# Attends drawn together, head sums in two float32r parts, an affine moved to ScalarE and two PSUM banks exchanged, in a hybrid decoder layer

## The chip, the cores and the metric

One core of a Trainium2 chip. The metric is the device time of one execution in microseconds (us); less is better. TensorE (PE) multiplies, PEld loads its stationary operands, VectorE (DVE), ScalarE (ACT) and GpSimd (POOL) work on elements, SyncE (SP) issues most of the DMAs. All run at the same time and wait for each other by semaphores.

## The reference

One decoder layer for 256 tokens of width 2048 in float32: a SwiGLU feed-forward part (5632 wide), a mixer of sliding-window attention beside RWKV-7 time mixing, cross-attention into 256 memory tokens, a second feed-forward part and a final norm. The change lies in the mixer, whose attention has 16 heads of 64, 4 key/value heads and blocks of 128, and whose time mixing has 16 heads of 64:

```python
def sliding_window_attention(q, k, v, sinks):
    ...
    s = jnp.einsum('bnqhgd,bnkhd->bnhgqk', qb, kb).astype(jnp.float32) * (HEAD_DIM ** -0.5)
    ...
    m = jnp.maximum(jnp.max(s, axis=-1, keepdims=True), sink)
    e = jnp.exp(s - m)
    p = e / (jnp.sum(e, axis=-1, keepdims=True) + jnp.exp(sink - m))
    o = jnp.einsum('bnhgqk,bnkhd->bnqhgd', p.astype(v.dtype), vb)

def rwkv7_time_mix(p, mu, w0, w2, a0, a2, g2, k_k, k_a, r_k, ln_w, ln_b):
    ...
    w_log = -jax.nn.softplus(-(w0.astype(f32) + jnp.tanh(xw) @ w2.astype(f32))) - 0.5
    a = jax.nn.sigmoid(a0.astype(f32) + xa @ a2.astype(f32))
    g = jax.nn.sigmoid(xg) @ g2.astype(f32)
    ...
    kk = k * k_k
    kk = kk / jnp.maximum(jnp.sqrt(jnp.sum(kk * kk, axis=-1, keepdims=True)), 1e-12)
    k = k * (1.0 + (a - 1.0) * k_a)
    y = rwkv7_scan(r, decay, k, v, -kk, kk * a)
```

kk are the removal keys; their squares are summed over each head's 64 columns.

## The kernel before

All weights stream from HBM through `load` (SP's DMAs). Each piece of 2x128 rows by 512 columns is split by ACT into a float32r part (`hi`, L365) and by DVE into the rest (`lo`, L366). Each product of a weight column block takes three float32r matmuls for each k and each 128 tokens: L442 (hi by hi), L443 and L444 (the two cross terms). These are the "plain" matmuls below; they fill most of the run. `product` issues them and calls `bg.tick()` between steps. The mixer's own work is written as generators in the queues of `Interleave`: at each tick every queue lets its first one or two generators run to their next `yield`, so `idle(n)` shifts work by n ticks. What a generator issues thus stands between plain matmuls in each engine's instruction order, and each engine runs its own order, one after the other.

PSUM has eight banks in three rings: `acc` (3, the products), `mm` (3) and `tr` (2, transposes and small results). A ring's bank is taken again when its last reader is done. SBUF tiles of the mixer come from a pool of 23 buffers (tag "t4").

The parts that the change touches, with the lines of before:

- `attend(kv)`, for each of four key/value heads, two at a time: scores (L954, query block 0 in two tr banks, block 1 in two mm banks) to tiles `s` (DVE, L962), maximum and exponential (ACT, L984), division (DVE, L993), transposes of the probabilities (L1003) through tr banks and ACT's copies to `pt` (L1007), output (L1014) in a tr bank, and its parts `yahi` (ACT, L1024) and `yalo` (DVE, L1025). For kv = 1 and 3 it idles five ticks first.
- `decay_and_rate`, when all four are done issuing ("attn"): it loads `wa`, the second rank weights of the decay and the rate, by two DMAs on POOL (L1078, L1079), applies Tanh and Sigmoid (L1081, L1082) to the small features xwa and xg, multiplies (L1091, mm and tr banks) and applies Sigmoid (L1098). The Sigmoid of xg also feeds DMAs of `gate_parts` on POOL (L1144), which copy rows of xg.
- `removal_keys(h)`, for each half of the heads: squares of kk on ACT (L1174), sums over a head by a matmul with block ones (L1179, float32), square root (ACT, L1180), maximum and reciprocal (DVE, L1182, L1184), the affine of the rate `aa` (DVE, L1202), products with it (L1206, L1207), and the masked products `lt` (L1224). `head_sums` (L906) is the helper that other sums use: two float32r matmuls, for a float32r part and the rest.
- the main stream beside it multiplies the gates and w_proj_attn and forms `ga` (DVE, L1271) from an acc bank.
- `pairs(h, q)`, the chunks of the recurrence (scores L1348, masks L1356, outputs L1459 and L1464), and `finish(h, i)` with the gate's product (L1523).

## Time and profile before

| what | value |
|---|---|
| median of three runs | 2225.18 us (2224.05 to 2226.93) |
| the profiled execution | 2226.33 us |
| its span in the profile | 2224.6 us |
| PE, DVE, ACT, POOL busy | 99%, 82%, 56%, 5% |
| HBM traffic | 209 GB/s over the span |

A row of the table by stretch holds the stretch and its length, then for PE, PEld, DVE, ACT and POOL the busy time and in brackets the instructions, then the granted clock of TensorE, the DMA engines' busy share and GB/s. A row of a timeline holds start, time (from the first's start to the last's end), engine, line, operation, output and input, tile size, shape and count; in brackets at its end the engine's idle time before it and what ended it. Matmuls overlap, so the distance between starts and not the time of one is what a matmul costs. A row of the waits holds the waiting group, what it waited for, total, number and longest, in us.

### The profile page before, as it was taken

What the parts mean: (1) busy time and instruction counts of PE and PEld (TensorE: products, weight loads), DVE (VectorE), ACT (ScalarE), POOL (GpSimd) and SP (SyncE); (2) the same over time, 40 slices, a digit from 0 to 9 for tenths busy, and PEclk for the clock granted to TensorE, in tenths of its full rate; (3) what the DMA queues carried; (4) which work ended last, traced back from release to release, by engine and by line L of the source; (5) the groups of instructions that cost most, each with busy time, mean ns of one, the idle gap of its engine ahead of it and who ended that gap; (6) DMA issues with size and microseconds to landing.
All of it is one profiled execution on the core that took longest, in us unless ns stands there. A gap on an engine that the chain in (4) does not pass through costs nothing.

```text
span 2224.6 us, 28133 instructions
## 1 busy us (share of the span) xinstructions
PE 2206.0 (99%) x10520; PEld 1819.2 (82%) x10520; DVE 1831.3 (82%) x2354; ACT 1244.2 (56%) x1611; POOL 107.2 (5%) x185
## 2 busy tenths in 40 slices
PE   9999999999999999999999999999999999999998
PEld 7888888888888877788888888888888888888886
DVE  7999988898989476978657666558999999999997
ACT  7555555555556467544544546556665565655654
POOL 0000000000000001000221030001000000000000
PEclk9999999999999999999999999999999999999999
DMA  8565555555556545676678678548565565656573
GB/s 304 194 209 198 194 203 199 201 191 202 203 192 202 175 126 149 191 235 209 205 236 293 203 265 281 186 157 288 206 234 189 197 247 204 208 208 218 199 242 137
DMA packets 231560, 466.02 MB, mean 209 GB/s; under 512 B 15520, under 2 KB 17920, under 8 KB 231424
## 3 DMA queue, kind: packets, MB, share of 16 engines
q1 hardware_dynamic: 222256, 438.08, 58.0%
q0 software_dynamic: 7648, 23.52, 3.5%
q10 hardware_dynamic: 1520, 2.63, 0.3%
q8 instruction: 82, 1.34, 0.2%
q14 instruction: 54, 0.44, 0.1%
HBM read 440.49 MB, written 23.59 MB: 209 GB/s over the span
## 4 chain that ended last, share of the span: by engine, by line
PE 94%; DVE 2%; DMA 1%; issue 1%; ACT 1%; SPq 0%; POOL 0%; POOLq 0%; DVEq 0%; ACTq 0%
PE acc L442 19%; PE acc L443 19%; PE acc L444 19%; PE mm L443 8%; PE mm L444 8%; PE mm L442 8%; PE tr L443 2%; PE tr L630 2%; PE tr L442 2%; PE tr L444 2%; PE mm L1418 1%; DVE lo L366 1%; DMA raw<-in_ffn_w_up_dram 0%; ACT hi L365 0%; DMA raw<-in_ffn_w_gate_dram 0%
## 5 line engine op out<-in xcount | busy, mean ns | idle before, releaser
L365 ACT CAST hi<-raw 128x1024 fp32r<-128x1024 f32 (+1 forms) x768 | 754.9, 993 | 698.3 <-PE acc L444 493.6
L366 DVE TENSOR_TENSOR lo<-raw,hi 128x1024 fp32r<-128x1024 f32 (+1 forms) x768 | 880.7, 1150 | 291.7 <-ACT hi L365 288.9
L442 PE MATMUL acc<-hi,xhi 128*128 128x512 f32 (+1 forms) x1134 | 448.1, 396 | 2.8 <-DVE ga L1271 1.3
L443 PE MATMUL acc<-lo,xhi 128*128 128x512 f32 (+1 forms) x1134 | 440.6, 389 | 0.8 <-DVE lo L366 0.8
L444 PE MATMUL acc<-hi,xlo 128*128 128x512 f32 (+1 forms) x1134 | 440.5, 389 | 0.0
L442 PEld LDWEIGHTS acc<-hi,xhi 128*128 128x128 f32 x1134 | 213.3, 188 | 49.2 <-issue 3.6
L443 PEld LDWEIGHTS acc<-lo,xhi 128*128 128x128 f32 x1134 | 213.6, 188 | 44.2 <-DVE lo L366 2.1
L444 PEld LDWEIGHTS acc<-hi,xlo 128*128 128x128 f32 x1134 | 213.2, 188 | 44.1 <-issue 0.8
L373 ACT CAST thi<-raw 128x1024 fp32r<-128x1024 f32 x192 | 200.2, 1051 | 67.5 <-DVE raw L396 44.1
L374 DVE TENSOR_TENSOR tlo<-raw,thi 128x1024 fp32r<-128x1024 f32 x192 | 232.5, 1219 | 0.9 <-ACT thi L373 0.3
L442 PE MATMUL mm<-hi,xhi 128*128 128x512 f32 x402 | 156.5, 389 | 0.0
L443 PE MATMUL mm<-lo,xhi 128*128 128x512 f32 x402 | 156.5, 389 | 0.0
L444 PE MATMUL mm<-hi,xlo 128*128 128x512 f32 x402 | 156.4, 389 | 0.0
L444 PE MATMUL acc<-hi,hlo 128*128 128x512 f32 x372 | 145.4, 391 | 0.0
L443 PE MATMUL acc<-lo,hhi 128*128 128x512 f32 x372 | 145.3, 391 | 0.0
L442 PE MATMUL acc<-hi,hhi 128*128 128x512 f32 x372 | 145.0, 390 | 0.0
L442 PEld LDWEIGHTS mm<-hi,xhi 128*128 128x128 f32 x402 | 75.5, 188 | 16.2 <-ACT hi L365 0.5
L443 PEld LDWEIGHTS mm<-lo,xhi 128*128 128x128 f32 x402 | 75.5, 188 | 15.8
L444 PEld LDWEIGHTS mm<-hi,xlo 128*128 128x128 f32 x402 | 75.5, 188 | 15.7
L442 PEld LDWEIGHTS acc<-hi,hhi 128*128 128x128 f32 x372 | 69.9, 188 | 14.3
L443 PEld LDWEIGHTS acc<-lo,hhi 128*128 128x128 f32 x372 | 69.8, 188 | 14.2
L444 PEld LDWEIGHTS acc<-hi,hlo 128*128 128x128 f32 x372 | 69.9, 188 | 14.1
(421 smaller groups left out, 3527.9 us busy)
## 6 DMA issues: line engine op xcount, KB each, us to landing
raw<-in_ffn_w_down_dram SPq DMA_DIRECT2D x88, 1024.0 KB, 5.2
raw<-in_ffn_w_gate_dram SPq DMA_DIRECT2D x84, 1024.0 KB, 5.0
raw<-in_ffn_w_up_dram SPq DMA_DIRECT2D x78, 1024.0 KB, 5.9
raw<-in_w_in_dram SPq DMA_DIRECT2D x136, 512.0 KB, 3.7
raw<-in_w_out_dram SPq DMA_DIRECT2D x32, 512.0 KB, 4.6
raw<-sums SPq DMA_DIRECT2D x20, 512.0 KB, 6.3
raw<-in_w_proj_attn_dram SPq DMA_DIRECT2D x16, 512.0 KB, 4.1
raw<-in_w_proj_rwkv_dram SPq DMA_DIRECT2D x16, 512.0 KB, 5.3
```

The lines of the kernel that those rows point to most:

```text
L365: at["hi"] = act.copy(hi[:, s], raw[:, s])
L366: at["lo"] = dve.tensor_tensor(lo[:, s], raw[:, s], f32(hi[:, s]), ALU.subtract)
L373: act.copy(hi[:], v[:])
L374: dve.tensor_tensor(lo[:], v[:], f32(hi[:]), ALU.subtract)
L442: pe.matmul(o, xh, hi, start=first, stop=False, **how)
L443: pe.matmul(o, xh, lo, start=False, stop=False, **how)
L444: pe.matmul(o, xl, hi, start=False, stop=last, **how)
L630: pe.transpose(b[:, o : o + P], tok[:, t, col : col + P], ident[:])
L1418: pe.matmul(vb[to, (o + k) * P : (o + k + 1) * P][:, r], lhs(k, e), v[:, k, r], start=v is u and k + e == 0, stop=True, **ek,)
```

## The change

Seven edits. `attend(3)` no longer idles five ticks (only kv = 1 does); ahead of the transposes attend(0) idles five ticks and the others three. The scores s of the first query block, which need half a buffer, and its probabilities pt share one t4 buffer, so that an attend takes three rather than four. `decay_and_rate` idles five ticks between the DMAs of wa and the Tanh. The sums of the squares take `head_sums`: ACT casts the squares to a float32r part, DVE forms the rest, and two float32r matmuls stand for one in float32. The affine of aa goes from DVE to ACT. One bank in `pairs` (h = q = 1, c = 0) and one in `finish(0, 0)` come from mm rather than tr, and `finish` idles one tick rather than two there.

```diff
--- before.py
+++ after.py
@@ -942,11 +942,16 @@
             if kv == 0:
                 with tc.issue_after(at["features"].ins):
                     act.activation(junk_t[:, :1], ones[:, :1], AF.Exp)
-            yield from idle(5 * (kv % 2))
+            yield from idle(5 * (kv == 1))
             s, b = [], []
             for qb, bank in enumerate((tr, mm)):
                 w, tq = P * (qb + 1), slice(qb * P, qb * P + P)
-                s.append(t4("s", (P, 2, 2, T)))
+                both = t4("s", (P, 2, 2, T))
+                if qb == 0:
+                    both = both[:].rearrange("p a b c -> p (a b c)")
+                    pt = [both[:, 4 * P :].rearrange("p (k i q) -> p k i q", k=1, i=4)]
+                    both = both[:, : 4 * P].rearrange("p (e c w) -> p e c w", e=2, c=2)
+                s.append(both)
                 b.append([bank() for _ in range(2)])
                 for c in range(2):
                     for e in range(2):
@@ -993,10 +998,9 @@
                     dve.tensor_scalar(
                         s3[qb][:, i], s3[qb][:, i], den[:, qb, i : i + 1], None, ALU.mult
                     )
-            yield from idle(3)
-            pt = []
+            yield from idle(5 if kv == 0 else 3)
+            pt.append(t4("pt", (P, 2, 4, P)))
             for qb in range(2):
-                pt.append(t4("pt", (P, 2, 4, P)))
                 for kb in range(qb + 1):
                     t_ = tr()
                     for i in range(4):
@@ -1077,6 +1081,7 @@
             wa = t4("wa", (P, RW))
             pool.dma_start(wa[0:64, :], W["rwkv_w2"])
             pool.dma_start(wa[64:128, :], W["rwkv_a2"])
+            yield from idle(5)
             with tc.issue_after(at["exp"].ins):
                 act.activation(xwa[0:64, :], xwa[0:64, :], AF.Tanh)
                 act.activation(xg[:], xg[:], AF.Sigmoid)
@@ -1166,17 +1171,19 @@
             yield from wait_for(f"k{h}")
             yield from wait_for("decay")
             ei = cs[h]
-            kk, sq = t4("kk"), t4("sq")
+            kk, sq, hi, lo = t4("kk"), t4("sq"), t4("sqhi", dt=F32R), t4("sqlo", dt=F32R)
             for i in range(4):
                 c = 4 * h + i
                 act.activation(kk[:, i, :], kt[h][:, i, :], AF.Copy, scale=nk_k[:, c : c + 1])
             yield
             act.activation(sq[:], kk[:], AF.Square)
+            halves_of(sq[:], hi[:], lo[:])
             yield
             for i in (0, 2):
-                b = tr()
                 sq2 = sq[:, i : i + 2, :].rearrange("p c t -> p (c t)")
-                pe.matmul(b[:], bdones[:], sq2, start=True, stop=True)
+                b = head_sums(
+                    bdones_r, [v[:, i : i + 2, :].rearrange("p c t -> p (c t)") for v in (hi, lo)]
+                )
                 act.activation(sq2, b[:], AF.Sqrt)
                 yield
                 dve.tensor_scalar(sq2, sq2, 1e-12, None, ALU.max)
@@ -1199,9 +1206,9 @@
             yield
             for i in range(4):
                 c = 4 * h + i
-                dve.tensor_scalar(
-                    aa[h][:, i, :], aa[h][:, i, :], k_a[:, c : c + 1], ok_a[:, c : c + 1],
-                    ALU.mult, ALU.add,
+                act.activation(
+                    aa[h][:, i, :], aa[h][:, i, :], AF.Identity, scale=k_a[:, c : c + 1],
+                    bias=ok_a[:, c : c + 1],
                 )
             dve.tensor_tensor(kt[h][:], kt[h][:], aa[h][:], ALU.mult)
             dve.tensor_tensor(aa[h][:], kt[h][:], ei[:], ALU.mult)
@@ -1446,7 +1453,7 @@
                 if c == 0:
                     mk_next = masked(scores(h, js, ((0, 1), (1, 1)), tr), mask3[:, :2])
                     yield
-                b = tr()
+                b = mm() if h == q == 1 and c == 0 else tr()
                 if c:
                     for k, j in enumerate(js):
                         pe.matmul(
@@ -1513,8 +1520,8 @@
             gl = sp.tile([P, 2 * P], F32R, tag="gl", name="gl", bufs=1)
             dve.tensor_tensor(gl[:], g2[:, 0, :], f32(gh[:, 0]), ALU.subtract)
             dve.tensor_tensor(gh[:64, 1], g2[:64, 1, :], f32(gh[:64, 1]), ALU.subtract)
-            yield from idle(2)
-            b = tr()
+            yield
+            b = mm() if h == i == 0 else tr()
             for k in range(2):
                 o, fk = b[:, k * T : (k + 1) * T], slice(k * P, (k + 1) * P)
                 for m, (g_, x_) in enumerate((
```

What this does to the order of the instructions, at three places. First, ACT around the Tanh of xwa and the Sigmoid of xg. Before, they stand between the copies of the last attend (pt, then its yahi):

```order
L1007 COPY pt<-tr 128x512
L1081 ACTIVATE xwa<-xwa 64x256
L1082 ACT_TABLE_LOAD
L1082 ACTIVATE xg<-xg 128x512
L1007 COPY pt<-tr 128x512 x2
L892 ACTIVATE tok<-acc,rs 128x512 x2
L365 CAST hi<-raw 128x1024
L1042 COPY p<-tr 128x2x256 x2
L1024 CAST yahi<-tr 128x512
L365 CAST hi<-raw 128x1024
L1098 ACTIVATE cs<-mm,cols 128x256 x2
```

With the change:

```order
L1011 COPY s<-tr 128x512
L1011 COPY pt<-tr 128x512
L365 CAST hi<-raw 128x1024
L1011 COPY pt<-tr 128x512
L1086 ACTIVATE xwa<-xwa 64x256
L1087 ACT_TABLE_LOAD
L1087 ACTIVATE xg<-xg 128x512
L1028 CAST yahi<-tr 128x512
L1011 COPY s<-tr 128x512
L365 CAST hi<-raw 128x1024
L1011 COPY pt<-tr 128x512 x2
L365 CAST hi<-raw 128x1024
```

The Tanh and the Sigmoid now stand ahead of the copies of attend(3) (s is its first query block), and of the yahi of attend(2). On POOL, whose queue holds wa's loads, before:

```order
L1144 DMA xg<-xg 32x256 x2
L1078 DMA wa<-in_rwkv_w_dram 64x1024
L1079 DMA wa<-in_rwkv_a_dram 64x1024
L1047 TENSOR_TENSOR d<-p 128x512 x2
L1144 DMA xg<-xg 32x256
L1040 MEMSET p 128x2 x2
L1047 TENSOR_TENSOR d<-p 128x512 x2
```

And with the change, on the same queue:

```order
L1149 DMA xg<-xg 32x256 x3
L1082 DMA wa<-in_rwkv_w_dram 64x1024
L1083 DMA wa<-in_rwkv_a_dram 64x1024
L1051 TENSOR_TENSOR d<-p 128x512 x2
L1044 MEMSET p 128x2 x2
L1051 TENSOR_TENSOR d<-p 128x512 x2
L1044 MEMSET p 128x2 x2
```

One more DMA of xg stands ahead of wa's two.

Second, PE from the output of attend(0) on. Before (L1014 is the output, L954 the scores; behind the arrow stand the two tiles read):

```order
L1014 MATMUL tr<-pt,vt 64x256 x6
L954 MATMUL tr<-kd,qt 128x128 x2
L442 MATMUL acc<-hi,xhi 128x288
L443 MATMUL acc<-lo,xhi 128x288
L444 MATMUL acc<-hi,xlo 128x288
L442 MATMUL acc<-hi,xhi 128x512
L443 MATMUL acc<-lo,xhi 128x512
L444 MATMUL acc<-hi,xlo 128x512
L442 MATMUL acc<-hi,xhi 128x512
L443 MATMUL acc<-lo,xhi 128x512
L444 MATMUL acc<-hi,xlo 128x512
```

With the change (L1018 is the output, L1007 the transposes, which were L1003):

```order
L1018 MATMUL tr<-s,vt 64x256 x2
L1018 MATMUL tr<-pt,vt 64x256 x4
L1007 MATMUL tr<-ident,s 128x128 x4
L444 MATMUL acc<-hi,xlo 128x288
L442 MATMUL acc<-hi,xhi 128x288
L443 MATMUL acc<-lo,xhi 128x288
L444 MATMUL acc<-hi,xlo 128x288
L442 MATMUL acc<-hi,xhi 128x512
L1007 MATMUL tr<-ident,s 128x128 x4
L443 MATMUL acc<-lo,xhi 128x512
L444 MATMUL acc<-hi,xlo 128x512
L1007 MATMUL tr<-ident,s 128x128 x4
```

The transposes of attend(1) now follow the output of attend(0) at once, and the scores of attend(2) after them: four turns of the tr ring where before plain matmuls stood.

Third, DVE in `removal_keys(0)` up to the first ga. Before:

```order
L1197 TENSOR_TENSOR kk<-kk,cs 128x1024
L1202 TENSOR_SCALAR aa<-aa,cols,ok_a 128x256 x4
L366 TENSOR_TENSOR lo<-raw,hi 128x1024
L1206 TENSOR_TENSOR kt<-kt,aa 128x1024
L1224 TENSOR_TENSOR lt<-tr,mask_l 128x512
L1207 TENSOR_TENSOR aa<-kt,cs 128x1024
L1224 TENSOR_TENSOR lt<-tr,mask_l 128x512
L1224 TENSOR_TENSOR lt<-mm,mask_l 128x512 x2
L1271 TENSOR_TENSOR ga<-acc,ga 128x512 x2
```

With the change (L1202 is here the product of kk and aa, which was L1195; L1213 and L1214 are what was L1206 and L1207):

```order
L1202 SCALAR_TENSOR_TENSOR kk<-kk,aa 128x1024
L366 TENSOR_TENSOR lo<-raw,hi 128x1024
L1204 TENSOR_TENSOR kk<-kk,cs 128x1024
L1213 TENSOR_TENSOR kt<-kt,aa 128x1024
L366 TENSOR_TENSOR lo<-raw,hi 128x1024
L1214 TENSOR_TENSOR aa<-kt,cs 128x1024
L1231 TENSOR_TENSOR lt<-tr,mask_l 128x512 x2
L1231 TENSOR_TENSOR lt<-mm,mask_l 128x512 x2
L1278 TENSOR_TENSOR ga<-acc,ga 128x512 x2
```

The four operations on aa are gone from DVE, and ga follows the masks as before.

## The prediction

> **What bounds the kernel now.** I read the page first, for how full TensorE (PE) is, then the table of busy time by stretch, the waits of PE, and the timeline around the longest wait.
>
> ```profile
> PE 2206.0 (99%) x10520; PEld 1819.2 (82%) x10520; DVE 1831.3 (82%) x2354; ACT 1244.2 (56%) x1611; POOL 107.2 (5%) x185
> ```
> ```profile
> 200.00:740.00 540.00, 540.00 (x2429) 446.79 (x2428) 486.33 (x602) 302.68 (x355) 8.31 (x29) 1.00 0.58 200
> 740.00:1400.00 660.00, 653.63 (x3564) 541.75 (x3563) 460.19 (x615) 346.92 (x525) 85.41 (x129) 0.99 0.67 214
> ```
> ```profile
> PE mm L1091 <- DMA wa<-in_rwkv_w_dram: 2.0, 1, 2.0
> PE tr L1003 <- DVE s L993: 1.6, 1, 1.6
> PE acc L442 <- DVE ga L1271: 1.3, 2, 0.7
> ...
> PE tr L1523 <- DVE mk L1356: 0.7, 1, 0.7
> ...
> PE tr L1459 <- DVE mk L1356: 0.3, 1, 0.3
> ```
>
> PE is busy in 2206.0 of 2224.6 us, so no change to another engine counts unless PE waits for it. In the first feed-forward part (200 to 740) PE has no idle time at all; in the mixer's stretch (740 to 1400), where every edit lies, it lacks 660 − 653.63 = 6.4 us and its mean granted clock is 0.99. So what can be won is PE's idle time there, PE's own work, and the clock. The waits name the five places. The largest is the load of wa, the rank weights of the decay and the rate:
>
> ```profile
> 844.42 0.49 PE L444 MATMUL acc<-hi,xlo 128*128 128x512 f32 x1
> 846.94 1.79 PE L1091 MATMUL mm<-xwa,wa 64*128 64x256 f32 x5 [2.03 <-DMA wa<-in_rwkv_w_dram]
> ...
> 855.01 0.40 PE L444 MATMUL acc<-hi,xlo 128*128 128x512 f32 x1
> ...
> 858.45 0.39 PE L444 MATMUL acc<-hi,xlo 128*128 128x512 f32 x1
> 858.77 1.13 PE L1091 MATMUL mm<-xwa,wa 64*128 64x256 f32 x8
> ...
> 861.04 0.40 PE L443 MATMUL acc<-lo,xhi 128*128 128x512 f32 x1
> ```
> ```profile
> 846.00:848.00 2.00, 1.06 (x6) 0.73 (x6) 1.23 (x1) 0.07 (x1) 0.00 (x0) 0.98 0.91 216
> 848.00:850.00 2.00, 2.00 (x10) 1.73 (x10) 1.27 (x2) 0.84 (x2) 0.00 (x0) 0.50 0.81 236
> ...
> 852.00:854.00 2.00, 2.00 (x6) 1.52 (x6) 2.00 (x6) 1.33 (x4) 0.20 (x2) 0.50 0.00 0
> 854.00:856.00 2.00, 2.00 (x9) 1.61 (x8) 1.84 (x4) 0.00 (x0) 0.00 (x0) 0.81 0.00 0
> ```
>
> The eighth column is the granted clock. After 2.03 us of idling PE starts again, and a microsecond later its clock is 0.50. From the two broken slices it is halved from 848 − 2×0.02/0.5 = 847.92 to 854 + 2×0.19/0.5 = 854.76, that is for 6.84 us, in which 3.4 us of work is lost. The busy share doesn't show this: a slow matmul counts as busy.
>
> What the place costs in all is read from its twin. Plain 128x512 matmuls run at (858.45 − 855.01)/15 = 0.229 us each. The second group of L1091 stands between the starts 858.45 and 861.04: 2.59 us for one L444, 16 L1091 and one L442. The first takes from 844.42 to 855.01, 10.59 us, for the same and seven plain matmuls more, which at full clock would be 2.59 + 7×0.229 = 4.19. So the place loses **6.4 us**: the wait, the half clock, and a short wait for wa's second half.
>
> **The change, part by part.**
>
> *The attention and wa.* Why wa is late:
>
> ```profile
> 836.35 0.59 ACT L1007 COPY pt<-tr 128x512 f32<-128x512 f32 x1
> ```
> ```profile
> 839.47 1.06 POOL L1144 DMA_DIRECT2D xg<-xg  x2 [24.57 <-ACT xg L1082]
> 840.52 0.53 POOL L1078 DMA_DIRECT2D wa<-in_rwkv_w_dram  x1
> 841.29 0.53 POOL L1079 DMA_DIRECT2D wa<-in_rwkv_a_dram  x1 [0.24 <-issue]
> ```
> ```profile
> DMA to landing us min/median/max: 6.4/6.5/6.6
> ```
>
> POOL's queue holds two DMAs of xg ahead of wa's, and they wait for ACT's sigmoid of xg. wa is issued at 840.52 and 841.29 and lands 6.4 and 6.6 us later, at 846.9 and 847.9. From the start of the copy of pt ahead of Tanh (836.35) to the second landing it is 11.5 us. The change leaves out the five idle steps of attend(3) (attend(0) gets two more), so that attends 2 and 3 follow closer, and Tanh and the sigmoid come out ahead of the last transposes of attend(3). On POOL three DMAs of xg now stand ahead of wa's rather than two: 0.53 more, 12.1 us from that copy to the landing. On PE there lie, from the transposes which that copy reads to the first L1096, 52 plain matmuls (52×0.229 = 11.9), 20 transposes of L1007 and L630, and twelve of L1018 (two groups as at 802.20). Their prices:
>
> ```profile
> 796.81 0.90 PE L1003 MATMUL tr<-ident,s 128*128 128x128 f32 x6
> 797.47 0.38 PE L442 MATMUL acc<-hi,xhi 128*128 128x288 f32 x1
> ...
> 802.20 1.52 PE L1014 MATMUL tr<-pt,vt 128*64 128x256 f32 x12 [0.44 <-ACT pt L1007]
> ```
>
> A transpose is 0.66/6 = 0.11 us, so 2.2 for twenty; the two groups are 2×1.52 = 3.0. That is 17.1 us against 12.1: wa has 5.0 us to spare, or 3.9 if the copy stands behind one weight cast of 1.05 us. On POOL these DMAs pass nothing that was ahead of them: the differences d of L1047 stood behind wa and still do, and the third xg DMA stood behind d. SP's loads of the weights are not passed, and the attends issue no DMA. The wait and its half clock go: **−6.4** (between −3, if the clock falls anyway, and −6.4).
>
> What is paid for it: attends 1 to 3 lie closer, and all of their transposes, scores and outputs go through the two "tr" banks, with fewer plain matmuls between. The 1.6 us before L1003 come ahead of anything that moved and stay, and so does the 0.44 at 802.20. In the rows shown for the second place L1007 wants the bank which the output of attend(0) leaves only when ACT and DVE have read it (0.585 + 0.69), and L959 wants one whose copy (0.59) stands behind a weight cast (1.05):
>
> ```profile
> L1024 ACT CAST yahi<-tr x4: 567/585/586, 803.8 to 844.5; 128x512 fp32r<-128x512 f32 x4
> ```
> ```profile
> 845.02 1.05 ACT L365 CAST hi<-raw 128x1024 fp32r<-128x1024 f32 x1
> ```
> ```profile
> 845.15 0.69 DVE L1025 TENSOR_TENSOR yalo<-tr,yahi 128x512 fp32r<-128x512 f32 x1 [1.66 <-ACT yahi L1024]
> ```
>
> The first is 1.28 us, against four transposes (0.44) and five plain matmuls (0.133 each for 288 columns, some 0.75): 0.1 is left. The second is 1.64 against four transposes and two plain ones, 0.44 + 0.46: 0.74 is left. Two or three more such turns have 0.1 or nothing. Behind a waiting transpose stand all of PE's matmuls. I take **+1.0**; the lower bound is 0, if the casts fall elsewhere, the upper 3.0, the uncovered 0.74 at each of four turns. That s and pt of the first query block share a buffer only removes a wait for a buffer; no row of PE's waits names one, so it counts 0.
>
> *Sums of squares.*
>
> ```profile
> 884.94 1.02 PE L1179 MATMUL tr<-sq,bdones 128*128 128x512 f32 x2
> 885.40 0.80 PE L442 MATMUL acc<-hi,xhi 128*128 128x512 f32 x1
> 886.03 0.40 PE L443 MATMUL acc<-lo,xhi 128*128 128x512 f32 x1
> ```
> ```profile
> L906 PE MATMUL tr<-kh,ones_r x4: 389/391/398, 1095.5 to 1144.1; 128*128 128x512 f32 x4
> ```
>
> The float32 product takes PE from 884.94 to 886.03 less one plain matmul: 1.09 − 0.23 = 0.86. The same helper's float32r product shows 0.391, as a plain matmul does (0.39 at a pitch of 0.229), so two are 0.46. Saved 0.40, four times: **−1.6**. Added for each half of the heads (h = 0, 1): a cast on ACT, 1.05 by the weight cast of the same 128x1024, and a subtraction on DVE, 1.2 by L366's of that size. PE's second product waits for the subtraction, with at most one plain matmul between the two, and all of PE stands behind it; behind the subtraction on DVE stands a weight's L366, which PE needs only two items later. A subtraction that has to let a L366 of 1.2 pass comes up to 1.2 − 2×0.23 = 0.75 late. I take **+0.4** (0 to 1.5, twice 0.75).
>
> *The affine of aa on ACT.*
>
> ```profile
> 912.28 1.06 ACT L365 CAST hi<-raw 128x1024 fp32r<-128x1024 f32 x1 [3.88 <-DVE lt L1224]
> 913.25 1.70 ACT L1172 ACTIVATE kk<-kt,nk_k 128x256 f32<-128x256 f32 x4
> ```
> ```profile
> 908.02 1.38 DVE L1202 TENSOR_SCALAR aa<-aa,cols,ok_a 128x256 f32<-128x256 f32 x4
> ...
> 915.11 1.28 DVE L1271 TENSOR_TENSOR ga<-acc,ga 128x512 f32<-128x512 f32 x2
> ```
> ```profile
> 914.81 0.39 PE L442 MATMUL acc<-hi,xhi 128*128 128x512 f32 x1
> 915.85 0.50 PE L442 MATMUL acc<-hi,xhi 128*128 128x512 f32 x1 [0.65 <-DVE ga L1271]
> ```
>
> DVE works without a gap from L1202 to ga, and PE's next product waits for ga's bank: 915.85 − 914.81 − 0.23 = 0.81. Without L1202 ga comes 1.38 sooner, more than this; the second such wait is alike. Both are 1.3 as idle time. ACT pays 1.7 for four of 128x256, by its L1172, and has an idle stretch of 3.88 just where L1202 stood; without that room DVE's product kt waits for it, and behind kt the lt masks and ga. I take **−1.3** (−1.6 with the excess of both; −0.5 if ACT's four end 0.8 later than DVE's did).
>
> *Two banks taken from mm.* They remove the waits of L1523 (0.7) and L1459 (0.3), which stand in the list above: −1.05. The mm banks have readers of their own, a copy (0.59) or a mask on DVE, and the scores that use mm next come one turn later, PE behind them: one third of a copy, 0.2, is my guess, and two whole ones, 1.2, the bound. **−0.85** (−1.05 to +0.15).
>
> Sum: −6.4 + 1.0 − 1.6 + 0.4 − 1.3 − 0.85 = −8.75. The profiled execution took 2226.33 (span 2224.6 and 1.7 around it), 1.15 above the median of the runs, 2225.18. From its own time: 2226.33 − 8.75 = **2217.6**.
>
> **The rivals.**
>
> *The clock falls anyway.* The half clock may come from the whole thin stretch of small matmuls around L1014 and L1091, not from the one wait. For it: 1.58 us of idling before L1003 left the clock at 1.00, and 2.03 is not much more. Against it: the mixer's other thin stretches kept their clock, since the 3.4 us lost here are 0.5% of the 660 and make up the whole 0.99. Then only the waits go, and 3.4 us stay: 2217.6 + 3.4 = 2221.0. [...]
>
> *wa is late again.* The change wouldn't do what it is for if Tanh slips behind further casts by more than the 3.9 us to spare. Then the 6.4 stay: 2224.0, within 0.2%.
>
> *The two tr banks lock.* The other side: from the output of attend(0) to the scores of attend(3) PE's rows take a tr bank eleven times. If each turn waits for its whole reader (1.28, as yahi and yalo), with a weight cast (1.05) ahead of every second one and only the plain matmuls of these rows to cover it (twelve of 0.229 and four of 0.133, 3.3), 14.1 + 5.3 − 3.3 = 16.1 are lost, and one gap past 2 us halves the clock (3.4): 19.5 in place of 1.0, so 2217.6 + 18.5 = 2236.1. It eats the whole gain from (8.75 + 1.0)/11 = 0.89 uncovered per turn. For it: 0.44 was waited for one pt copy in a looser order. Against it: before, too, four attends pass the same banks, and only that wait is in PE's list.
>
> *The moved work comes late*: sqlo at 1.5, aa at −0.5, the mm banks at +0.15 and the turns at 3.0: 2217.6 + 1.1 + 0.8 + 1.0 + 2.0 = 2222.5.
>
> **How the numbers follow.** Forecast 0.70; clock falls anyway 0.08; wa late 0.07; banks lock 0.06; moved work late 0.09. The low bounds of the terms (−6.4, 0, −1.6, 0, −1.6, −1.05) give −10.65, and with the 1.15 between the profiled execution and the median 2214.5; 2213.5 leaves 1 us for a wait that I didn't see go. Upwards the range takes in the late work, 2222.5. The forecast's own range is 2214.5 to 2220.7. What a measurement of this kernel can tell from no change is about 0.2%, here 4.45 us, so faster means under 2220.7. The forecast lies below it, and the first rival on it, half to each side: faster 0.70 + 0.04 + 0.04 of the late work (where only a part of it comes late) = 0.78; same 0.04 + 0.07 + 0.05 = 0.16; slower 0.06.
>
> **What would show it.** Right: no wait for wa in PE's list, the clock at 1.00 from 200 to 1400, wa issued some 4 us ahead of its need; ga, L1523's and L1459's successors gone from the waits; two L906 of 0.39 in place of each L1179. New short waits of tr for ACT's pt or DVE's yalo between 800 and 830, none above 1 us. Wrong: a wait over 2 us among those, followed by slices at 0.50; wa in the list; PE waiting for sqlo, or ACT's L1209 as the reason of a DVE wait with PE behind it.

## The result and the profile after

The change takes 2218.29 us (median of 7 runs, 2216.97 to 2218.49) against 2226.51 (7 runs, 2221.94 to 2228.11) for the kernel before: a ratio of 0.9966 with a 95% interval of 0.9955 to 0.9977. The forecast was 2217.6 us, faster. The execution profiled took 2216.97 with a span of 2215.2.

The page's busy time and the waits of PE in the changed kernel (waiting group, releaser, total, number, longest, in us):

```profile
PE 2200.2 (99%) x10520; PEld 1817.0 (82%) x10520; DVE 1829.0 (83%) x2348; ACT 1250.0 (56%) x1621; POOL 107.0 (5%) x185
```
```profile
PE tr L1007 <- DVE s L998: 1.6, 1, 1.6
PE acc L442 <- DVE ga L1278: 1.5, 2, 0.9
...
PE tr L1018 <- ACT pt L1011: 0.3, 1, 0.3
...
PE tr L1223 <- DVE kk L1204: 0.2, 1, 0.2
```

The wait for wa is gone, and so are those of L1523 and L1459. The waits for ga, which were to go, stand at 1.5 rather than 1.3, and L1223 has a new one. The mixer's stretch in the table by stretch, with the granted clock in the eighth column:

```profile
740.00:1400.00 660.00, 656.38 (x3603) 546.50 (x3603) 462.65 (x614) 358.52 (x544) 85.21 (x129) 1.00 0.68 217
```

PE now lacks 3.6 us there rather than 6.4, at a clock of 1.00. PE around wa's products, in its timeline:

```profile
842.32 0.40 PE L444 MATMUL acc<-hi,xlo 128*128 128x512 f32 x1
842.64 1.13 PE L1096 MATMUL mm<-xwa,wa 64*128 64x256 f32 x8
843.61 1.03 PE L1096 MATMUL tr<-xwa,wa 64*128 64x256 f32 x8
844.57 0.50 PE L442 MATMUL acc<-hi,xhi 128*128 128x512 f32 x1
844.91 0.40 PE L443 MATMUL acc<-lo,xhi 128*128 128x512 f32 x1
```

From the L444 to the L443 it is 2.59 us, to the hundredth what its twin took before. POOL's timeline, and the landing of wa's DMAs in the view of that tile:

```profile
828.73 1.55 POOL L1149 DMA_DIRECT2D xg<-xg  x3 [10.47 <-ACT xg L1087]
830.52 0.53 POOL L1082 DMA_DIRECT2D wa<-in_rwkv_w_dram  x1 [0.24 <-PE tr L1007]
831.04 0.53 POOL L1083 DMA_DIRECT2D wa<-in_rwkv_a_dram  x1
```
```profile
DMA to landing us min/median/max: 3.7/4.0/4.2
```

wa lands at 831.04 + 4.2 = 835.2 at the latest, 7.4 us before PE wants it; 3.9 to 5.0 were predicted, with the landing time of before, 6.4 to 6.6. The path on PE was right: from the copy of pt ahead of Tanh (825.61) to wa's first product it took 17.0 us, where 17.1 were predicted.

Between any two of the marks below all kernels have the same plain matmuls (up to 54 of the 8928 stand in exchanged places), so the time of PE between two marks can be compared. The marks are, in the kernel before: the first transposes of the attention (start 795.44), the last plain matmul ahead of wa's first products (844.42), the first behind its second products (860.70), the first product with the attention's output (898.99), the first of its last column block (1005.33), and the first with the time mixing's output (1279.72). In us, each kernel less the profiled execution of before:

| kernel | attention | wa | sums, first half | second half, aa, ga | values to time mixing |
|---|---|---|---|---|---|
| the change | −1.04 | −6.42 | −0.73 | −0.42 | −0.52 |
| the change, second profile | −1.04 | −6.42 | −0.74 | −0.44 | −0.53 |
| predicted | +1.0 | −6.4 | −0.6 | −1.9 | −0.85 |
| wa_early | −0.01 | −6.14 | 0.00 | 0.01 | −0.04 |
| attn_only | −1.03 | −6.42 | −0.05 | −0.01 | −0.09 |
| sums_only | −0.02 | −3.70 | −0.70 | 0.12 | −0.11 |
| aa_only | −0.04 | −0.73 | −0.05 | −0.52 | −0.07 |
| banks_only | −0.04 | −0.42 | −0.05 | 0.01 | −0.55 |
| kt_last | −1.03 | −6.42 | −0.73 | −0.26 | +5.15 |
| wa_later | −0.02 | −4.94 | −0.05 | 0.01 | −0.10 |
| bank_one | 0.03 | −0.20 | 0.00 | 0.01 | −0.14 |
| buf4 | −1.53 | −6.43 | −0.67 | −0.45 | −0.53 |
| pool_kt | −1.03 | −6.42 | −0.70 | −1.82 | −0.55 |
| pool_kt_again | −1.02 | −6.42 | −0.74 | −1.81 | −0.53 |

The stretches of the change sum to −9.13 (predicted −8.75). Ahead of them the profiled execution of the change had won 1.06 us, 0.9 of it in the first 31 us, and behind them it lost 0.87; both vary from profile to profile of one kernel and belong to no edit: the two profiles of pool_kt have spans of 2215.2 and 2213.7 us with the same sum of stretches, −10.52.

### The profile page after: what moved, and what is told of

Read it like the earlier page. It is cut to its first block, busy times and chain, and to the rows that moved or that the text cites. A ratio compares the mean times of both kernels' runs of the same rounds, so it can differ in the third digit from the quotient of the medians.

```text
span 2215.2 us, 28140 instructions
## 1 busy us (share of the span) xinstructions
PE 2200.2 (99%) x10520; PEld 1817.0 (82%) x10520; DVE 1829.0 (83%) x2348; ACT 1250.0 (56%) x1621; POOL 107.0 (5%) x185
## 4 chain that ended last, share of the span: by engine, by line
PE 94%; DVE 3%; DMA 1%; issue 1%; ACT 1%; SPq 0%; POOLq 0%; POOL 0%; DVEq 0%; ACTq 0%
PE acc L442 19%; PE acc L443 19%; PE acc L444 19%; PE mm L443 8%; PE mm L444 8%; PE mm L442 8%; PE tr L443 2%; PE tr L630 2%; PE tr L442 2%; PE tr L444 2%; PE mm L1425 1%; DVE lo L366 1%; DMA raw<-in_ffn_w_up_dram 1%; PE tr L1355 0%; ACT hi L365 0%
## 5 line engine op out<-in xcount | busy, mean ns | idle before, releaser
L366 DVE TENSOR_TENSOR lo<-raw,hi 128x1024 fp32r<-128x1024 f32 (+1 forms) x768 | 878.8, 1147 | 291.8 <-ACT hi L365 289.3
L442 PE MATMUL acc<-hi,xhi 128*128 128x512 f32 (+1 forms) x1134 | 445.7, 394 | 2.0 <-DVE ga L1278 1.5
L443 PE MATMUL acc<-lo,xhi 128*128 128x512 f32 (+1 forms) x1134 | 439.9, 388 | 0.8 <-DVE lo L366 0.8
L444 PE MATMUL acc<-hi,xlo 128*128 128x512 f32 (+1 forms) x1134 | 439.7, 388 | 0.0
L442 PEld LDWEIGHTS acc<-hi,xhi 128*128 128x128 f32 x1134 | 213.2, 188 | 47.8 <-issue 3.1
L444 PEld LDWEIGHTS acc<-hi,xlo 128*128 128x128 f32 x1134 | 212.9, 188 | 43.5 <-issue 0.4
L443 PEld LDWEIGHTS acc<-lo,xhi 128*128 128x128 f32 x1134 | 213.4, 188 | 42.7 <-DVE lo L366 2.2
L442 PE MATMUL mm<-hi,xhi 128*128 128x512 f32 x402 | 156.6, 389 | 0.1
L443 PE MATMUL mm<-lo,xhi 128*128 128x512 f32 x402 | 156.5, 389 | 0.0
L444 PE MATMUL mm<-hi,xlo 128*128 128x512 f32 x402 | 156.4, 389 | 0.0
L444 PE MATMUL acc<-hi,hlo 128*128 128x512 f32 x372 | 145.4, 391 | 0.0
L443 PE MATMUL acc<-lo,hhi 128*128 128x512 f32 x372 | 145.3, 391 | 0.0
L442 PE MATMUL acc<-hi,hhi 128*128 128x512 f32 x372 | 145.0, 390 | 0.0
L442 PEld LDWEIGHTS mm<-hi,xhi 128*128 128x128 f32 x402 | 75.4, 188 | 16.2 <-ACT hi L365 0.5
L443 PEld LDWEIGHTS mm<-lo,xhi 128*128 128x128 f32 x402 | 75.5, 188 | 15.8
L444 PEld LDWEIGHTS mm<-hi,xlo 128*128 128x128 f32 x402 | 75.5, 188 | 15.7
L442 PEld LDWEIGHTS acc<-hi,hhi 128*128 128x128 f32 x372 | 69.9, 188 | 14.3
L443 PEld LDWEIGHTS acc<-lo,hhi 128*128 128x128 f32 x372 | 69.8, 188 | 14.3
L444 PEld LDWEIGHTS acc<-hi,hlo 128*128 128x128 f32 x372 | 69.9, 188 | 14.0
```

The source lines that it names most:

```text
L366: at["lo"] = dve.tensor_tensor(lo[:, s], raw[:, s], f32(hi[:, s]), ALU.subtract)
L442: pe.matmul(o, xh, hi, start=first, stop=False, **how)
L443: pe.matmul(o, xh, lo, start=False, stop=False, **how)
L444: pe.matmul(o, xl, hi, start=False, stop=last, **how)
```

## The experiments

Each part of the change alone, on the kernel before, and then parts on the change. The medians of the kernels that keep the wait for wa (sums_only, aa_only, banks_only, bank_one) mix executions with a mean granted clock of 0.997 or 0.998 and others with 0.999; in the kernel before these are some 3 us apart, as explained further on. What a part is worth is therefore read from the stretches and not from the medians.

**wa_early**: wa alone. PE's order is that of before, row by row.

```diff
+            wa = t4("wa", (P, RW))
+            pool.dma_start(wa[0:64, :], W["rwkv_w2"])
+            pool.dma_start(wa[64:128, :], W["rwkv_a2"])
             yield from wait_for("attn")
-            wa = t4("wa", (P, RW))
-            pool.dma_start(wa[0:64, :], W["rwkv_w2"])
-            pool.dma_start(wa[64:128, :], W["rwkv_a2"])
```

> Before with one edit: the two DMAs of wa are issued on POOL ahead of the wait for the attention, so ahead of the DMAs of xg; PE's order is the same as before, row by row. If the late wa alone made the wait and the half clock, the wait of L1091 is gone, the clock stays at 1.00, the first L1091 group costs 2.59 as its twin does, and the profiled span is 6.4 us shorter (2218.2). If the thin stretch of small matmuls lowered the clock by itself, the clock still falls to 0.50 there and only 3.0 us go. If the other load of the stretch took over, under 1 us goes.

Measured: 2220.80 us (11 runs, 2220.27 to 2221.91), ratio 0.9982 (0.9974 to 0.9991), span 2218.5. The place costs 6.14 us less, and the slices from 836 to 858 are at a granted clock of 1.00. Its timeline:

```profile
843.91 0.49 PE L444 MATMUL acc<-hi,xlo 128*128 128x512 f32 x1
844.34 1.13 PE L1091 MATMUL mm<-xwa,wa 64*128 64x256 f32 x8
845.30 1.22 PE L1091 MATMUL tr<-xwa,wa 64*128 64x256 f32 x8
846.45 0.50 PE L442 MATMUL acc<-hi,xhi 128*128 128x512 f32 x1
```

With the same thin stretch of small matmuls, but without the wait, the mean clock is 0.999 in all of its 11 executions. So the first rival falls in the form in which it stood: the thin stretch alone does not do it.

**attn_only**: the attention's edits, the shared buffer and the idle steps alone.

```diff
-            yield from idle(5 * (kv % 2))
+            yield from idle(5 * (kv == 1))
...
-            yield from idle(3)
+            yield from idle(5 if kv == 0 else 3)
...
             pool.dma_start(wa[64:128, :], W["rwkv_a2"])
+            yield from idle(5)
```

> Before with the edits of the attention, its buffer and the idle steps alone. Trace of the change: from the first transposes to wa's first product PE was 1.0 us quicker, and at wa 6.4. If both come from these edits alone, PE reaches the second group of L1096 7.4 us sooner than before, and the span is 7.4 shorter. If tr banks cost 1.0, as predicted, and the other edits hid it, 5.4.

Measured: 2219.49 us (10 runs, 2219.07 to 2220.90), ratio 0.9975 (0.9966 to 0.9984). Both gains, −1.03 and −6.42, come from these edits. They are 1.3 us under wa_early, and 1.03 of that is the attention's own. The predicted cost of 1.0 doesn't exist.

**sums_only**: the sums of squares alone (the diff's first hunk in `removal_keys`).

```diff
-                pe.matmul(b[:], bdones[:], sq2, start=True, stop=True)
+                b = head_sums(
+                    bdones_r, [v[:, i : i + 2, :].rearrange("p c t -> p (c t)") for v in (hi, lo)]
+                )
```

> Before with the sums of squares in two float32r parts alone. PE's own work falls by 4 x 0.41 = 1.6. If DVE is the limit from the sums to ga, its two added subtractions (1.2 each) are paid back at ga: the wait of L442 for ga grows from 0.65 and 0.62 to about 1.5 each, and the span is about the same (-1.6 + 1.8). If the subtractions are hidden, the waits for ga stay at 1.3 in all and the span is 1.6 shorter.

Measured: 2223.56 us (11 runs, 2221.31 to 2228.13), ratio 0.9998 (0.9990 to 1.0007). The first half of the heads wins 0.70, and with the second half, where the waits for ga also lie, 0.12 is lost: 0.58 in all rather than 1.6 (1.2 with the predicted cost of the subtractions). The waits:

```profile
PE acc L442 <- DVE ga L1273: 2.0, 2, 1.2
...
PE mm L1091 <- DMA wa<-in_rwkv_w_dram: 1.5, 1, 1.5
```

ga's grew from 1.3 to 2.0, which points to the first of the two theories, DVE as the limit, at less than its full size. The table's −3.70 at wa is no effect of the sums; it is taken up below.

**aa_only**: the affine of aa on ACT alone.

```diff
-                dve.tensor_scalar(
+                act.activation(
```

> Before with the affine of aa on ACT alone. If DVE is the limit up to ga, the 1.4 us taken off it end both waits for ga (1.3 idle, 1.6 with the restart) and the span is 1.3 to 1.6 shorter. If the order puts another weight's L366 ahead of ga in its place, or DVE waits for ACT's affine, the waits stay within 0.3 of 1.3 and so does the span.

Measured: 2225.32 us (11 runs, 2222.42 to 2227.54), ratio 1.0002 (0.9993 to 1.0011). One of the two waits for ga is left, of 0.7; the stretches win 0.57 rather than 1.3. Neither theory has it wholly: the second wait went, and the first didn't. PE's timeline, from the end of L1216's products to the first:

```profile
909.55 0.50 PE L444 MATMUL acc<-hi,yalo 128*128 128x512 f32 x1
...
912.63 0.39 PE L442 MATMUL acc<-hi,xhi 128*128 128x512 f32 x1
913.73 0.50 PE L442 MATMUL acc<-hi,xhi 128*128 128x512 f32 x1 [0.71 <-DVE ga L1271]
```

14 plain matmuls stand there ahead of the product that waits; in the kernel before there are 20 (910.36 to 914.81). PE's order has moved, though the edit touches only ACT and DVE. On the kernel before the sums and the affine give −0.58 and −0.57, and together in the change −1.15: they add up, so neither hides the other.

**pool_kt**: is it DVE's load ahead of ga? The change with two products of aa on POOL.

```diff
-            dve.tensor_tensor(kt[h][:], kt[h][:], aa[h][:], ALU.mult)
-            dve.tensor_tensor(aa[h][:], kt[h][:], ei[:], ALU.mult)
+            pool.tensor_tensor(kt[h][:], kt[h][:], aa[h][:], ALU.mult)
+            pool.tensor_tensor(aa[h][:], kt[h][:], ei[:], ALU.mult)
```

> The change with the products L1213 and L1214 on POOL rather than DVE. If DVE's load ahead of ga is what PE waits for, 2.4 us less of it end both waits for ga: 1.5 to 2 us shorter. If POOL's products (some 2.5 each, after L1047's 1.25 for half the size) hold up its DMAs of the masked products, the substitution starts later and PE meets that wait later instead: nothing won.

Measured: 2216.58 us (5 runs, 2216.36 to 2217.03), ratio to before 0.9962 (0.9950 to 0.9975). The stretch with ga is 1.40 us shorter than in the change, and of the waits for ga one of 0.5 is left:

```profile
PE acc L442 <- DVE ga L1278: 0.5, 1, 0.5
```

So it is DVE's queue that PE meets at ga. Its timeline in the change itself:

```profile
898.14 1.21 DVE L1204 TENSOR_TENSOR kk<-kk,cs 128x1024 f32<-128x1024 f32 x1
899.28 1.22 DVE L1213 TENSOR_TENSOR kt<-kt,aa 128x1024 f32<-128x1024 f32 x1
900.41 1.21 DVE L366 TENSOR_TENSOR lo<-raw,hi 128x1024 fp32r<-128x1024 f32 x1
901.55 1.22 DVE L1214 TENSOR_TENSOR aa<-kt,cs 128x1024 f32<-128x1024 f32 x1
902.68 1.28 DVE L1231 TENSOR_TENSOR lt<-tr,mask_l 128x512 f32<-128x512 f32 x2
903.88 1.27 DVE L1231 TENSOR_TENSOR lt<-mm,mask_l 128x512 f32<-128x512 f32 x2
905.08 1.27 DVE L1278 TENSOR_TENSOR ga<-acc,ga 128x512 f32<-128x512 f32 x2
```
```profile
904.87 0.39 PE L442 MATMUL acc<-hi,xhi 128*128 128x512 f32 x1
905.81 0.50 PE L442 MATMUL acc<-hi,xhi 128*128 128x512 f32 x1 [0.55 <-DVE ga L1278]
```

There is no gap from L1204 to this ga, as there was none from L1202 before, and PE arrives in time to wait. (Ahead of the second ga DVE does idle, 0.84 us at 933.66, for ACT's cast.) In pool_kt the order counts beside the load: the first multiplication of ga runs at 900.83 there, ahead of the masks, and the first wait is gone.

**kt_last**: another way to the same end, the affine and both products put behind the masks.

```diff
-            for i in range(4):
-                c = 4 * h + i
-                act.activation(
-                    aa[h][:, i, :], aa[h][:, i, :], AF.Identity, scale=k_a[:, c : c + 1],
...
                 pool.dma_start(ld[:, o : o + 8, :], lt[:])
                 yield
+            for i in range(4):
+                c = 4 * h + i
+                act.activation(
+                    aa[h][:, i, :], aa[h][:, i, :], AF.Identity, scale=k_a[:, c : c + 1],
```

> The change with the affine of aa and the two products with it (L1213, L1214) moved behind the masked products lt in removal_keys. If DVE's order ahead of ga makes PE wait there, the first half of ga's multiplication comes ahead of the masks, both waits for ga (1.5 in all) go, and the stretch from the first yahi to w_proj_attn's last part is 1.5 to 2 us shorter. If DVE is simply full in this stretch, ga's second half waits instead and less than 0.5 is won.

Measured: 2225.68 us (11 runs, 2223.41 to 2227.40), ratio 0.9997 (0.9988 to 1.0006); the change's whole gain is gone. Part of that goes with the clock, whose mean is 0.997 or 0.998 in 6 of the 11; these have a median of 2225.73, the five at 0.999 one of 2223.87. The waits for ga did go from the list, but a new one of 1.7 for ACT's cast came in their stretch (the other wait in this line, of 0.8, lies outside the mixer):

```profile
PE acc L442 <- ACT hi L365: 2.5, 2, 1.7
```

In the stretch behind it, up to the time mixing's output, it takes 5.7 us more than the change. 1.3 of these are new waits, the longest of 0.9; the rest is PE's own time, with the small matmuls of the pairs in 59 groups between plain ones rather than 51. That the generator's two extra steps moved the pairs is the likely cause, but no run has these steps alone. A miss: the work was moved past more than it was meant to pass.

**banks_only** and **bank_one**: both banks, and that of `finish` alone, on the kernel before.

```diff
-                b = tr()
+                b = mm() if h == q == 1 and c == 0 else tr()
...
-            yield from idle(2)
-            b = tr()
+            yield
+            b = mm() if h == i == 0 else tr()
```

(bank_one has the second piece only.)

> Before with the two banks from mm and one idle step less alone. In the trace of the change the stretch from w_proj_attn's last part to w_proj_rwkv lost only 0.5 us, against 0.85 predicted and 1.05 of waits gone. If this comes from these edits, the stretch is 0.4 to 0.6 shorter here too, with the waits of L1523 and L1459 gone from the list and other matmuls of the stretch dearer. If the rest was lost to the other edits, it is 1.0 to 1.4 shorter.

> Before with the bank of finish(0, 0) from mm and one idle step less, without the bank in pairs. The stretch from w_proj_attn's last part to w_proj_rwkv was 0.55 shorter with both. If the bank of finish alone gave its wait of 0.74 (0.9 with the restart) back further on, and the gain is that of the bank in pairs, this stretch is within 0.15 of before, with L1459's wait of 0.3 still there; if each pays in part, 0.2 to 0.5 shorter.

Measured: 2224.87 us (11 runs, 2222.11 to 2226.65), ratio 1.0000 (0.9991 to 1.0008); and 2226.26 (11 runs, 2223.29 to 2228.47), ratio 1.0005 (0.9996 to 1.0014). The stretch is 0.55 and 0.14 shorter. The bank of `finish` takes away a wait of 0.74 and wins 0.14, the bank in `pairs` one of 0.31 and wins the other 0.4. L1459's wait is still in bank_one's list:

```profile
PE tr L1459 <- DVE mk L1356: 0.3, 1, 0.3
```

So `finish` gives most of its wait back between its product and the next chunk; the small matmuls of the pairs then lie in other groups. With both banks 1.05 us of waiting goes and 0.55 is won, so PE's own time in the stretch rises by 0.5. Which matmuls became dearer I can't name from the rows.

**buf4**: the change with four buffers per attend.

```diff
-                both = t4("s", (P, 2, 2, T))
-                if qb == 0:
-                    both = both[:].rearrange("p a b c -> p (a b c)")
...
-                s.append(both)
+                s.append(t4("s", (P, 2, 2, T)))
```

> The change with four t4 buffers for an attend, as before, rather than three. If the shared buffer only removes a wait for a buffer that PE never met, the attention's stretch stays within 0.3 us of the change's and the time within 0.5. If the order of the attends rests on it, PE meets new waits for tr or for t4 there and loses the 1.0 us which that stretch gained.

Measured: 2217.54 us (7 runs, 2217.26 to 2218.81), ratio 0.9970 (0.9958 to 0.9981), against 2217.90 for the change on the same chip. The sharing isn't needed for the time; without it the attention's stretch is even 0.5 shorter, which no theory had; in the time it doesn't show.

**wa_later**: does the length of the wait decide whether the clock falls?

```diff
             wa = t4("wa", (P, RW))
+            pool.memset(wa[:], 0.0)
```

> Before with a memset of wa on POOL and a third DMA of xg ahead of wa's DMAs, so that they are issued some 1.5 to 2 us later; L1091 comes in more pieces. In the runs so far waits of 1.3 to 2.0 us went with the clock falling in about half the executions (mean granted clock 0.997 to 0.998) and staying in the others (0.999). If the length of the wait decides, a wait of 3 us or more lowers the clock in every execution: all at 0.998 or less, some 3 us above the slowest of before. If only the moment decides, executions at 0.999 still occur as often.

Measured: 2223.00 us (11 runs, 2220.85 to 2223.55), ratio 0.9990 (0.9981 to 0.9999), all at a clock of 0.999. The run doesn't answer. Three more plain matmuls stand ahead of wa's first products, some 0.7 us, and the DMAs, issued at 842.18 and 842.71, landed within 3.8 to 4.4 us, so that the wait became shorter and not longer:

```profile
PE mm L1092 <- DMA wa<-in_rwkv_w_dram: 0.3, 1, 0.3
```

**after_again** and **pool_kt_again**, on one chip.

> The change itself, unchanged, beside the next kernels on one chip. In 10 executions the clock stays at 0.999, since PE has no wait for wa: within 1.5 us of 2218.3. If the clock depends on the chip or on chance alone, some at 0.998 or less, 3 us longer.

> The change with L1213 and L1214 on POOL once more, to be compared with the change on the same chip. If the 1.4 us which its trace gained between the first yahi and w_proj_attn's last part is its whole effect, its median is 1.2 to 1.8 below that of the change; if it is given back behind it, within 0.5.

Measured: 2217.90 us (6 runs, 2217.57 to 2219.02), ratio 0.9972 (0.9960 to 0.9983); and 2217.28 (5 runs, 2215.44 to 2218.17), ratio 0.9968 (0.9955 to 0.9980). pool_kt's trace wins the same 1.4 again in its stretch, but the median on this chip is only 0.62 lower than the change's, between the two forecasts. Over both sittings its ten runs have a median of 2216.98 and the thirteen of the change one of 2217.96: about 1.0 us lower, with spreads that overlap.

## Why the prediction was right, step by step

**wa, −6.4: right in mechanism and size** (−6.42; wa_early −6.14 for the load alone). The twin was a good measure. What I had not seen is that the kernel before does not lose it each time. In 77 further executions of before the mean granted clock is 0.997 or 0.998 in 37 and 0.999 in 40, with medians of 2226.43 and 2223.56 us. sums_only and aa_only show both kinds with waits of 1.49 and 1.26 us. In the timelines and the table by stretch of sums_only first, then of aa_only (granted clock in the eighth column):

```profile
846.20 1.13 PE L1091 MATMUL mm<-xwa,wa 64*128 64x256 f32 x4 [1.49 <-DMA wa<-in_rwkv_w_dram]
```
```profile
848.00:850.00 2.00, 2.00 (x11) 1.46 (x11) 1.74 (x3) 1.31 (x5) 0.00 (x0) 1.00 0.81 238
```
```profile
846.15 1.13 PE L1091 MATMUL mm<-xwa,wa 64*128 64x256 f32 x4 [1.26 <-DMA wa<-in_rwkv_w_dram]
```
```profile
848.00:850.00 2.00, 2.00 (x10) 1.62 (x7) 1.09 (x2) 0.33 (x2) 0.00 (x0) 0.50 0.76 205
```

The shorter wait lost the clock, the longer one kept it. That is why the table's column for wa reads −3.70 for the one and −0.73 for the other, though neither kernel touches wa: the difference, 3.0, is nearly the 3.4 us that the prediction put on the half clock alone.

The length of the wait doesn't tell the two kinds apart in these traces. In the kernel before PE waits from 844.91 to 846.94, and the clock is then at 0.50 for 6.84 us by its slices. In aa_only it waits from 844.89 to 846.15, and by the slices (0.91 in 846 to 848, 0.50 up to 854, 0.89 in 854 to 856) the half clock lasts 6.8 us. In sums_only it waits from 844.71 to 846.20, and all slices from 836 to 858 are at 1.00. banks_only and bank_one wait 1.4 us each; their profiled executions have a mean clock of 0.997, and at this place they are only 0.42 and 0.20 us under the kernel before. And in the kernel before the wait of 1.58 ahead of the first transposes leaves the slices from 792 to 800 at 1.00. What decides is not shown: no run changes the place of the wait alone. That one gap past 2 us halves the clock, as the rival with the tr banks has it, rested on the single wait of 2.03; in aa_only 1.26 us went with a half clock as long, and in sums_only 1.49 with none.

The prediction stood because its sum was made against one execution, whose clock had fallen; the gain between medians rests on the share of such executions. Against the 77, whose median is 2224.69, the change wins 6.4 us rather than the 8.2 of the first comparison.

**The attention, +1.0: wrong, −1.04.** The step that failed is "Two or three more such turns have 0.1 or nothing … I take +1.0": it counted what a tr bank waits for, and nothing else. The turns I had priced at 0.74 don't wait. PE's timeline of the change there:

```profile
804.11 0.49 PE L443 MATMUL acc<-lo,xhi 128*128 128x512 f32 x1
804.44 0.40 PE L444 MATMUL acc<-hi,xlo 128*128 128x512 f32 x1
804.68 0.60 PE L1007 MATMUL tr<-ident,s 128*128 128x128 f32 x4
805.20 0.71 PE L959 MATMUL tr<-kd,qt 64*128 64x128 f32 x4
805.84 0.50 PE L442 MATMUL acc<-hi,xhi 128*128 128x512 f32 x1
```

L959 follows L1007 by 0.52 us, four transposes of 0.11 and no idle time. And it left out what moving costs or wins in itself. The group of small matmuls at wa costs more than its matmuls: its 2.59 us are one L444, one L442 (0.229 each) and 16 products at (843.61 − 842.64)/8 = 0.121, which is 2.40, so 0.19 go into entering and leaving it. From the first transposes to wa's products the order of before has 25 such groups and that of the change 19, with as many small matmuls (142): at the price of that one group, which is an estimate for the others, 6×0.19 = 1.1. PE's idle time there is 0.09 less, so 1.2 in all against 1.04 measured. buf4 has 18 groups and is 0.49 shorter still. That this is the cause is argued from the rows and the count; no run had the groups alone changed. And the count isn't the whole price: from the attention's last column block to the time mixing's output banks_only has 51 groups rather than 54 and 1.05 us less waiting, and wins only 0.55.

**The sums, −1.6 + 0.4: right on PE, but half of it isn't won** (−0.58 alone, where −1.2 were predicted). PE's timeline of the change, at both sums of the first half:

```profile
876.37 0.39 PE L906 MATMUL tr<-sqhi,ones_r 128*128 128x512 f32 x1
876.59 0.39 PE L442 MATMUL acc<-hi,xhi 128*128 128x512 f32 x1
876.91 0.50 PE L906 MATMUL tr<-sqlo,ones_r 128*128 128x512 f32 x1
877.24 0.39 PE L443 MATMUL acc<-lo,xhi 128*128 128x512 f32 x1
...
883.85 0.39 PE L906 MATMUL tr<-sqhi,ones_r 128*128 128x512 f32 x1
884.07 0.39 PE L906 MATMUL tr<-sqlo,ones_r 128*128 128x512 f32 x1
884.30 0.39 PE L442 MATMUL acc<-hi,xhi 128*128 128x512 f32 x1
```

The first costs 877.24 − 876.37 − 0.23 = 0.64, the second 884.30 − 883.85 = 0.45, as predicted (0.46); the second half has 0.62 and 0.45. In the two dearer ones the load of the second product's stationary operand (PEld) waits 0.35 and 0.31 us for DVE's subtraction. Four times 0.86 less these 2.16 is 1.28, so what PE saves came out as summed. The step that failed is to count all of it as won, although PE waits for ga further on. Counted from the mark behind wa's second products, PE comes to the first ga 0.71 us sooner in sums_only than before, and ga itself only 0.19 sooner; the wait grows from 0.65 to 1.16. The sums don't relieve DVE, on which ga stands: they add a subtraction of 1.22, which goes into time in which DVE idled before (2.41 us of idling between the sums and ga, 1.15 in sums_only).

**The affine, −1.3: the step that failed is "Without L1202 ga comes 1.38 sooner, more than this".** ga did come sooner. The first wait for it ends 913.73 − 859.94 = 53.79 us behind the mark after wa's second products in aa_only, and 915.85 − 860.70 = 55.15 in the kernel before: 1.36 sooner. But in PE's order the product that takes ga's bank moved forward by the six plain matmuls counted above, 6×0.229 = 1.37, so the first wait stayed (0.71 for 0.65) and nothing was won there. At the second the wait went, which is the 0.57. The change has the same order at its first ga (14 plain matmuls and a wait of 0.55); at the second PE comes 1.50 sooner than before and waits 0.91. The sums and the affine together give −1.15, where −2.5 were predicted. The prediction held PE's order fixed; what moved it is open. That DVE's queue sets the rest pool_kt shows: with two products off DVE the stretch wins 1.4 more.

**The banks, −0.85: mis-sized, −0.52**, by what the bank of `finish` gives back.

So the total came right because two errors met: the attention was 2.0 us better than predicted, the work around DVE and the banks 1.7 worse. Of the rivals, "the clock falls anyway" and "wa is late again" fell with wa_early and the trace after, and the lock of the tr banks with the rows above. The moved work came late only in small, by the 0.35 and 0.31 for which PEld waits for the subtraction.

## What to carry to other kernels

What one engine saves ahead of a wait for another is won only as far as the other comes sooner too: of the 1.28 us that the sums save on PE, sums_only won 0.58. So price all edits ahead of one wait together, on both engines. An edit on one engine can also move the order on another, as in aa_only, where 14 plain matmuls stood ahead of the waiting product rather than 20: compare the orders before taking a wait as gone. Where small matmuls interrupt a stream of long ones, their order had a price here even where nothing waited, 0.19 us for the group at wa; the number of interruptions is a hint at it, not a measure. Before comparing medians, look at the granted clock of every execution: here a wait of 1.26 us went with 6.8 us at half the clock in one trace, and one of 1.49 with none in another.

## What the runs showed of the hardware

- Waits of 1.3 to 2.0 us ahead of wa's products were followed by a clock of 0.50 for 6.8 us in the traces of the kernel before and aa_only, went with a mean clock of 0.997 in those of banks_only and bank_one, and left it at 1.00 in that of sums_only; of 77 executions of the kernel before 37 have a mean clock of 0.997 or 0.998, the others 0.999. The wait of 1.6 us before the first transposes came without a lower clock: the six kernels that have it, with at most 0.3 of waiting for wa and no new wait above 0.5 in the mixer (the change, wa_early, attn_only, pool_kt, buf4, wa_later), ran 62 times, always at 0.999. What tells the two places apart is open.
- The DMAs of wa took 5.6 to 6.6 us to land when issued between 840 and 843 in the five kernels that wait for them, and 3.4 to 4.2 in the kernels that issue them before 834. The moment alone isn't the reason: in wa_later, issued at 842.18 and 842.71, they took 3.8 to 4.4.
- The products L1213 and L1214 of 128x1024 took 1.22 us each on DVE in the change, and 2.38 and 3.27 on POOL in pool_kt, where the DVE subtraction beside the first took longer too. In pool_kt, POOL's timeline, then DVE's:

```profile
900.64 2.38 POOL L1213 TENSOR_TENSOR kt<-kt,aa 128x1024 f32<-128x1024 f32 x1 [24.92 <-DMA raw<-in_w_in_dram]
903.10 3.27 POOL L1214 TENSOR_TENSOR aa<-kt,cs 128x1024 f32<-128x1024 f32 x1
```
```profile
901.54 2.57 DVE L366 TENSOR_TENSOR lo<-raw,hi 128x1024 fp32r<-128x1024 f32 x1
```

  The L366 took 2.57 rather than 1.22 us and ended 1.09 us behind the end of L1213. The masked products beside L1214, with one operand in PSUM, took 1.28 and 1.27 for two each, as in the change.
